# HGRN2's f, q, g and the two gates' projections in seven block products, with the quadrant sums of the input made at HGRN2's start

## The chip, the cores and the metric

The kernel runs on one core of one Trainium2 chip. The metric is the device time of one execution in microseconds (us), the median of several runs. TensorE (PE) does the matmuls and the transposes, VectorE (DVE) and ScalarE (ACT) the elementwise work, GpSimd (POOL) a few small or spare ones, and SyncE (SP) issues all DMAs in one queue, in order.

## The reference, cut to what matters

One block of a network on 512 tokens of width 1024: a SwiGLU feed-forward stage (FFN1), then two mixers side by side on the same normalized input n, HGRN2 (a gated linear recurrence of 8 heads) and a Mamba-2 SSD, joined by two sigmoid gates, then a second feed-forward stage (FFN2), an embedding gate and a norm. What the change touches:

```python
n = rms_norm(h, mix_norm[l])
hq, hf, hi, hgate, mz, mxbc, mdt, br_gates = jnp.split(n @ w_in[l], split_at, axis=-1)
o_hg = hgrn2_recurrence(hq, hf, hi, lower_bounds[l])
o_hg = rms_norm(o_hg, hg_norm[l].reshape(HG_HEADS, HG_DV)).reshape(b_, s_, HG_VDIM)
o_hg = (o_hg * jax.nn.silu(hgate.astype(f32))).astype(h.dtype)
...
gate_a, gate_b = jnp.split(jax.nn.sigmoid(br_gates), 2, axis=-1)
mixed = gate_a * (o_hg @ w_hg_out[l]) + gate_b * (y @ w_ssm_out[l])
h = h + mixed @ w_out[l]
```

hq, hf and hgate (q, f and g below) are 1024 columns each, br_gates 2048. All of it is float32.

## The kernel before

**Matmuls.** Every float32 operand is kept as a pair of float32r blocks, hi and lo. `split` makes the pair: an ACT cast (L507) for hi and a DVE subtraction (L508) for lo. `mm` makes three matmuls of it, hi·hi, hi·lo and lo·hi (L502 to L504). Weights come by DMA (L458) in chunks and are split on the chip, each once; the normalized input n2 is split once and stays (class `Act`).

**Two forms of a projection.** f, q, g, the two gates GA and GB, and ho (the product with `w_hg_out`) use `tile`: 128 output columns by all 512 tokens, eight steps over D = 1024, so 24 matmuls of 128x512 into one PSUM bank. FFN1 and FFN2 use `Seven` instead: four such tiles are computed together as a 2 by 2 block product in seven products of quadrants instead of eight (Strassen and Winograd's form). The seven are a·e, b·g, S4·h, d·T4, S1·T1, S2·T2 and S3·T3, where a, b, c, d are quadrants of the weights, e, f, g, h of the input, S1 to S4 are sums of weight quadrants that DVE makes for each group (L492 to L495, each 128x1024), and T1 to T4 sums of input quadrants that are made once. A product has 24 matmuls of 128x256. `take` gathers the seven results: ACT copies (L851) and DVE adds (L854, L858, L861). A group of `Seven` also has seven weight blocks to split where four tiles have four.

**Order.** `Block.run` goes through a list of units in order. Each unit first loads and splits the weights of units ahead, as far as its six numbers (`AHEAD`, `AHEAD_GATES`, ...: two distances in units of work, one for raw loads, and the blocks to leave spare for each) and the free blocks of the SBUF arena allow (48 blocks, 46 of them of 4 KB a partition). Then it issues its matmuls, and after each piece of them a step of every background generator (`slot`). `pair_gen` is such a generator: the elementwise work and small matmuls of one pair of heads, with decay factors made on POOL (L1243 to L1252), the factored operands on DVE (L1281 to L1284), attention blocks (L1296, L1298, L1305), state (L1316), norm (L1326 to L1332) and a transpose (L1338) that DVE multiplies by the gate (L1339). Each engine executes its instructions in the order that results, and waits on semaphores of the others.

**The stages.** After the SSD's last part come HGRN2's four head pairs: the value projection v (for two pairs at once), then f, q, g of each pair (`HG.plan`; copied out of PSUM by ACT at L1192), then eight tiles of GA (sigmoid L1477), eight of GB (sigmoid L1483, product L1484) and eight of ho (L1491, L1492 and a split), then `w_out` and FFN2.

## Time and profile before

| | us |
|---|---|
| median of 3 runs | 1606.13 (1604.15 to 1610.71) |
| the profiled execution, its own time | 1607.06 |
| its span, first to last instruction | 1605.4 |
| PE busy in the span | 1567.4 (98%) |
| DVE busy | 1001.5 (62%) |
| ACT busy | 717.5 (45%) |
| POOL busy | 203.8 (13%) |

The mean granted TensorE clock of the core is 0.992. ACT's copies of f, q and g (L1192) start between 794.8 and 1010.3 us; the gates run from about 1011 to 1117 us, ho to 1157 us. "Busy" of an engine is the time in which at least one of its instructions executes; a row of a timeline or a group carries the engine, the line of the kernel, the operation, what it writes and reads, and what it waited for in square brackets. Neighbouring instructions on an engine overlap in part, so the cost of one in a row of many is the distance of two starts, not its duration.

### The profile page before, as it was taken

What the parts mean: (1) busy time and instruction counts of PE and PEld (TensorE: products, weight loads), DVE (VectorE), ACT (ScalarE), POOL (GpSimd) and SP (SyncE); (2) the same over time, 40 slices, a digit from 0 to 9 for tenths busy, and PEclk for the clock granted to TensorE, in tenths of its full rate; (3) what the DMA queues carried; (4) which work ended last, traced back from release to release, by engine and by line L of the source; (5) the groups of instructions that cost most, each with busy time, mean ns of one, the idle gap of its engine ahead of it and who ended that gap; (6) DMA issues with size and microseconds to landing.
All of it is one profiled execution on the core that took longest, in us unless ns stands there. A gap on an engine that the chain in (4) does not pass through costs nothing.

```text
span 1605.4 us, 22240 instructions
## 1 busy us (share of the span) xinstructions
PE 1567.4 (98%) x9054; PEld 1362.4 (85%) x9054; DVE 1001.5 (62%) x1223; ACT 717.5 (45%) x1070; POOL 203.8 (13%) x258
## 2 busy tenths in 40 slices
PE   8999999999999899999999999999999999999997
PEld 7999999988877678787878887888889999999986
DVE  7877767665565455667445652644448876877653
ACT  6544544445453444354454353433136543444532
POOL 1000000000044241536211010200000000000000
...
GB/s 272 138 92 108 117 92 79 106 178 189 60 80 63 128 101 142 111 222 100 138 67 112 163 46 48 119 143 92 103 70 116 118 119 80 109 102 85 211 47 53
DMA packets 192044, 181.48 MB, mean 113 GB/s; under 512 B 6804, under 2 KB 155940, under 8 KB 191940
## 3 DMA queue, kind: packets, MB, share of 16 engines
...
HBM read 165.27 MB, written 14.75 MB: 112 GB/s over the span
## 4 chain that ended last, share of the span: by engine, by line
PE 88%; DMA 3%; DVE 3%; POOL 2%; issue 2%; ACT 1%; SPq 0%; POOLq 0%; DVEq 0%; ACTq 0%
PE bank L502 27%; PE bank L504 27%; PE bank L503 27%; DMA blk<-cscr 1%; PE bank L1076 1%; PE bank L1296 1%; PE bank L529 1%; DMA accscr<-blk 1%; DMA blk<-in_x_dram 1%; ACT blk L507 0%; DMA blk<-in_w_in_dram 0%; DVE blk L508 0%; POOL blk L1057 0%; PE bank L1070 0%; POOL blk L1061 0%
## 5 line engine op out<-in xcount | busy, mean ns | idle before, releaser
L502 PE MATMUL bank<-blk,blk 128*128 128x512 f32 (+1 forms) x2648 | 912.3, 347 | 18.2 <-DVE blk L508 9.2
L503 PE MATMUL bank<-blk,blk 128*128 128x512 f32 (+1 forms) x2648 | 909.4, 344 | 0.8 <-DVE blk L508 0.8
L504 PE MATMUL bank<-blk,blk 128*128 128x512 f32 (+1 forms) x2648 | 905.0, 344 | 0.0
L508 DVE TENSOR_TENSOR blk<-blk,blk 128x1024 fp32r<-128x1024 f32 (+2 forms) x461 | 457.3, 1017 | 252.2 <-ACT blk L507 148.2
L502 PEld LDWEIGHTS bank<-blk,blk 128*128 128x128 f32 x2648 | 503.8, 191 | 76.7 <-DVE blk L508 10.5
L507 ACT CAST blk<-blk 128x1024 fp32r<-128x1024 f32 (+2 forms) x461 | 389.6, 879 | 368.0 <-PE bank L503 100.7
L503 PEld LDWEIGHTS bank<-blk,blk 128*128 128x128 f32 x2648 | 504.6, 191 | 55.3 <-DVE blk L508 1.0
L504 PEld LDWEIGHTS bank<-blk,blk 128*128 128x128 f32 x2648 | 502.4, 190 | 53.5 <-issue 0.2
L538 POOL TENSOR_SCALAR small<-small 128x1 f32<-128x1 f32 (+1 forms) x40 | 9.9, 248 | 992.3 <-ACT blk L544 859.3
L851 ACT COPY blk<-bank 128x512 f32<-128x512 f32 x80 | 46.9, 586 | 129.0 <-PE bank L504 129.0
L739 DVE SCALAR_TENSOR_TENSOR blk<-bank,blk 128x512 f32<-128x512 f32 x80 | 54.9, 686 | 30.1 <-PE bank L504 29.5
L955 DVE SCALAR_TENSOR_TENSOR blk<-bank,small,blk 128x511 f32<-128x511 f32 (+2 forms) x72 | 53.6, 744 | 15.8 <-ACT blk L953 14.8
L1076 PEld LDWEIGHTS bank<-blk,blk 128*128 128x128 f32 x256 | 42.4, 198 | 9.1 <-issue 5.5
L1036 DVE TENSOR_TENSOR blk<-blk,blk 128x1024 f32<-128x1024 f32 x16 | 22.9, 1432 | 39.5 <-POOL blk L1034 39.5
L492 DVE TENSOR_TENSOR blk<-blk,blk 128x1024 f32<-128x1024 f32 x20 | 24.4, 1221 | 30.6 <-PE bank L503 15.6
L507 ACT CAST blk<-bank 128x256 fp32r<-128x256 f32 x68 | 23.4, 374 | 35.8 <-PE bank L529 35.6
L1076 PE MATMUL bank<-blk,blk 128*128 128x64 f32 x256 | 38.3, 264 | 0.0
L508 DVE TENSOR_TENSOR blk<-bank,blk 128x256 fp32r<-128x256 f32 x68 | 26.9, 417 | 14.1 <-ACT blk L507 13.8
L731 ACT ACTIVATE blk<-blk 128x512 f32<-128x512 f32 x40 | 25.2, 630 | 20.7 <-DVE blk L854 15.1
L1112 DVE SCALAR_TENSOR_TENSOR blk<-blk,small,blk 128x512 f32<-128x512 f32 x16 | 14.8, 926 | 30.1 <-POOL small L539 20.9
L1037 ACT ACTIVATE blk<-blk 128x1024 f32<-128x1024 f32 x16 | 17.0, 1061 | 36.6 <-DVE blk L1036 32.8
L1034 POOL TENSOR_SCALAR_AFFINE_SELECT blk<-blk 128x1024 f32<-128x1024 f32 x16 | 21.2, 1323 | 95.2 <-DMA blk<-cscr 94.4
...
## 6 DMA issues: line engine op xcount, KB each, us to landing
blk<-in_ffn_w_dram SPq DMA_DIRECT2D x132, 512.0 KB, 4.4
blk<-in_w_in_dram SPq DMA_DIRECT2D x89, 512.0 KB, 3.8
blk<-in_w_ssm_out_dram SPq DMA_DIRECT2D x16, 512.0 KB, 3.9
blk<-cscr SPq DMA_DIRECT2D x16, 512.0 KB, 6.0
...
blk<-in_w_hg_out_dram SPq DMA_DIRECT2D x8, 512.0 KB, 3.5
blk<-in_w_out_dram SPq DMA_DIRECT2D x8, 512.0 KB, 3.9
```

The source lines that it names most:

```text
L492: v.tensor_tensor(s["S1"], q["c"], q["d"], ALU.add)
L502: t.matmul(out, lhsT=lh, rhs=rh, start=start, stop=False, skip_group_check=more)
L503: t.matmul(out, lhsT=lh, rhs=rl, start=False, stop=False, skip_group_check=more)
L504: t.matmul(out, lhsT=ll, rhs=rh, start=False, stop=stop, skip_group_check=more)
L507: self.nc.scalar.copy(hi, src)
L508: self.nc.vector.tensor_tensor(lo, src, hi.bitcast(F32), ALU.subtract)
L731: act(c, c, AF.Silu)
L739: v.scalar_tensor_tensor(hd, bank, 0.5, hd, ALU.mult, ALU.add)
L851: b.nc.scalar.copy(st[p], bank)
L955: nc.vector.scalar_tensor_tensor(t[:, s:], pc[:, 0:T - s], b.cw[:, 3 - s, ct:ct + 1], t[:, s:], ALU.mult, ALU.add)
L1036: v.tensor_tensor(R[j], R[j], self.cc[:, j, gh][:, :, None].broadcast_to([P, HPG, P]), ALU.subtract)
L1076: nc.tensor.matmul(pyv[:, hh, :], lhsT=R[c][:, hh, :], rhs=xdt[:, hh, :], start=True, stop=True)
```

## The change

- **T1 to T4 for n2.** `ActS`, a new class, adds the four sums of n2's quadrants as operand pairs: eight more blocks that stay until the gates end. The generator `sums` makes them as HGRN2 begins, from the pairs that are there (four additions of 128x1024, eight subtractions of 128x512 and eight splits of 128x512). Before that, `KEEP` = 8 blocks are held free (`reserve`).
- **f, q, g.** f and q of a pair are one group of `Seven`, g of two pairs another: six groups instead of 24 tiles. A pair's generator starts when all four of its inputs are there.
- **The gates.** Two tiles of GA and the two of GB with the same place form a group: four groups instead of 16 tiles. `gates_done` works on halves of the tokens (256), and so does `ho_done`.
- **Lookahead.** HGRN2's units get (6, 10, 16, 2, 4, 4) and the gates' and ho's (6, 10, 16, 2, 3, 3).

Ten groups of `Seven` take the place of 40 tiles. Weights, loads and results are the same in number and size, but a load is now half the depth by 256 columns (128x4x256). Lines of helpers move down by 37 to 41 (L502 to L504 become L539 to L541, L507 and L508 L544 and L545, L492 to L495 L529 to L532, L458 L495).

```diff
-AHEAD_GATES = (2, 6, 8, 4, 8, 8)
+AHEAD_HG = (6, 10, 16, 2, 4, 4)
+AHEAD_GATES = (6, 10, 16, 2, 3, 3)
...
+class ActS(Act):
+    def sums(self):
+        b, v = self.b, self.b.nc.vector
+        self.op = {k: b.pair(4, T // 2) for k in ("T1", "T2", "T3", "T4")}
+        b.reserve = 0
+        for i in range(2):
+            full = []
+            for hi, lo in (self.blocks[i], self.blocks[i + 2]):
+                full.append(b.t(2, T))
+                v.tensor_tensor(full[-1], hi.bitcast(F32), lo.bitcast(F32), ALU.add)
+            yield 1
...
+            for r, x, y, n in ((t, h, f, "T3"), (f, f, e, "T1"), (f, h, f, "T2"), (g, g, f, "T4")):
+                v.tensor_tensor(r, x, y, ALU.subtract)
+                b.split(r, *[z[:, 2 * i:2 * i + 2] for z in self.op[n]])
...
+    def seven(self, w, c0, c1, act, done, pace):
+        ch = Chunk(w, 0, KD, c0, 4 * P, "w", c1)
+        q = Seven(self, act, done)
+        return [Unit([next(x for x in ch.halves if x.j == PRODUCTS[p][0])], lambda wt, p=p: q.product(wt, p, pace))
+                for p in ORDER]
...
-        for nme, off in (("f", OFF_F), ("q", OFF_Q), ("g", OFF_G)):
-            res += b.tiles(Chunk(b.i["w_in"], 0, KD, off + hp * 256, 256, "c"), self.n,
-                           lambda j, bank, nme=nme: made(j, bank, nme), HG_PACE)
+        res += b.seven(w, OFF_F + hp * 256, OFF_Q + hp * 256, self.n, made((st, "f"), (st, "q")), HG_PACE)
+        if hp % 2 == 0:
+            nxt = self.st[hp + 1]
+            res += b.seven(w, OFF_G + hp * 256, OFF_G + hp * 256 + 256, self.n, made((st, "g"), (nxt, "g")), HG_PACE)
...
     def hg_begin():
         hg.begin()
+        b.start("sums", n2[0].sums())
...
+    def gates_done(o, A, d):
+        for j in range(2):
+            acc[d + j] = b.t(T)
+            nc.sync.dma_start(acc[d + j], ssd.scr_acc[d + j])
+        for th in range(2):
+            nc.scalar.activation(o[th], o[th], AF.Sigmoid)
+            s_[d, th] = o[th]
+        for th, y in ((1, o[3]), (0, None)):
+            x = b.t(2, 256) if y is None else y
+            nc.scalar.activation(x, A if y is None else y, AF.Sigmoid)
+            for j in range(2):
+                a = acc[d + j][:, th * 256:th * 256 + 256]
+                nc.vector.tensor_tensor(a, a, x[:, j], ALU.mult)
+            b.fr(x)
...
+    for d in range(0, KD, 2):
+        U.extend(b.seven(ins["w_in"], OFF_GA + d * P, OFF_GB + d * P, n2, lambda o, A, d=d: gates_done(o, A, d), GATE_PACE))
```

**DVE, where the gates begin and the last pair of heads (6 and 7) is worked on.** A row is the line, the operation, what it writes and reads, the size, and the engines that it waits for. Before, this is the pair's chain from an L1284 on, with two weight splits (the L508 of 128x1024):

```order
L1284 TENSOR_TENSOR blk4_6226<-blk8_6755,small_63 128x512 [waits DVE_49,Pool_49]
L1330 TENSOR_REDUCE small_63<-blk6_6379 128x4 [waits Activation_49]
L1283 TENSOR_TENSOR blk5_7563<-blk16_7433,small_63 128x384 [waits PE_49]
L1284 TENSOR_TENSOR blk5_7563<-blk8_6755,small_63 128x512
L1257 SCALAR_TENSOR_TENSOR blk11_7136<-blk11_7136,blk10_7268 128x1024 [waits Activation_49]
L1332 TENSOR_TENSOR blk6_6379<-bank1_65,small_63 128x512 [waits DVE_49,Pool_49]
L508 TENSOR_TENSOR blk35_6496<-blk18_7133,blk26_6938 128x1024 [waits DMAHW2_49,PE_49,Activation_49]
L508 TENSOR_TENSOR blk7_7270<-blk10_7268,blk19_6497 128x1024 [waits DMAHW3_49,PE_49,Activation_49]
L1339 SCALAR_TENSOR_TENSOR blk6_6379<-bank4_68,small_63,blk36_6868 128x512 [waits DVE_49,PE_49]
L1283 TENSOR_TENSOR blk36_6868<-blk16_7433,small_63 128x384 [waits DVE_49]
L508 TENSOR_TENSOR blk21_7052<-blk6_6379,blk21_7052 128x512 [waits Activation_49]
```

In the changed kernel the chain begins at the transposed head (L1395) and runs to the split of a group's S1 (`blk23_7791`, an addition made 29 rows earlier), the lo part of which is `blk46_8081`:

```order
L1395 SCALAR_TENSOR_TENSOR blk26_7018<-bank2_66,small_63,blk46_7197 128x512 [waits DVE_49,PE_49]
L1284 TENSOR_TENSOR blk37_8024<-blk20_8002 128x1024 [waits DVE_49]
L1285 TENSOR_TENSOR blk27_8023<-blk20_8002 128x1024
L545 TENSOR_TENSOR blk21_8062<-blk26_7018,blk21_8062 128x512 [waits Activation_49]
L1310 TENSOR_TENSOR blk37_8024<-blk37_8024,blk17_7473 128x1024 [waits Activation_49]
L1311 SCALAR_TENSOR_TENSOR blk20_8002<-blk20_8002,blk5_7716 128x1024 [waits Activation_49]
L1337 TENSOR_TENSOR blk41_174<-blk37_8024,small_63 128x512 [waits DVE_49,Pool_49]
L1337 TENSOR_TENSOR blk1_6543<-blk37_8024,small_63 128x512
L1312 TENSOR_TENSOR blk15_7682<-blk15_7682,blk17_7473 128x1024 [waits Activation_49]
L1340 TENSOR_TENSOR blk1_6543<-blk20_8002,small_63 128x512 [waits DVE_49,Pool_49]
L545 TENSOR_TENSOR blk46_8081<-blk23_7791,blk26_8080 128x1024 [waits Activation_49]
```

More of the pair's chain now stands between a read of PE's transposes and the next weight split: ten operations ahead of the split of S1 here, where two weight splits came right behind L1257 and L1332 before.

**PE, at the same place.** Before, one split of a weight block (`blk7_7270` is the lo part) is followed by 24 matmuls of 128x512; these are the last of the tile before and the first of it:

```order
L504 MATMUL bank6_70<-blk29_1940,blk35_6496 128x512
L502 MATMUL bank7_71<-blk45_3214,blk19_6497 128x512
L503 MATMUL bank7_71<-blk42_3215,blk19_6497 128x512
L504 MATMUL bank7_71<-blk45_3214,blk7_7270 128x512
L502 MATMUL bank7_71<-blk45_3214,blk19_6497 128x512
L503 MATMUL bank7_71<-blk42_3215,blk19_6497 128x512
L504 MATMUL bank7_71<-blk45_3214,blk7_7270 128x512
L502 MATMUL bank7_71<-blk24_2460,blk19_6497 128x512
L503 MATMUL bank7_71<-blk28_122,blk19_6497 128x512
```

In the changed kernel, from the transposes that DVE's L1395 reads (`bank2_66`) to the first matmul that reads `blk46_8081`; the rows left out are eleven matmuls of 128x256 of lines L539 to L541 that wait for nothing:

```order
L1394 MATMUL bank2_66<-small_63,blk26_7018 128x128 [waits DVE_49]
L1394 MATMUL bank2_66<-small_63,blk26_7018 128x128 x3
L541 MATMUL bank1_65<-blk13_104,blk35_7957 128x256
L539 MATMUL bank1_65<-blk13_104,blk18_5830 128x256
...
L539 MATMUL bank1_65<-blk47_5006,blk34_7353 128x256 [waits Activation_49]
L540 MATMUL bank1_65<-blk4_4974,blk34_7353 128x256
L1352 MATMUL bank6_70<-blk20_8002,blk37_8024 32x32 [waits DVE_49]
L539 MATMUL bank4_68<-blk3_1180,blk26_8080 128x256 [waits Activation_49]
L540 MATMUL bank4_68<-blk7_4870,blk26_8080 128x256
L1347 MATMUL bank5_69<-small_63,blk41_174 128x128 [waits DVE_49]
L1347 MATMUL bank5_69<-small_63,blk41_174 128x128 x2
L541 MATMUL bank4_68<-blk3_1180,blk46_8081 128x256 [waits DVE_49]
```

Between the two stand 17 matmuls of 128x256, one of 32x32 and three transposes of 128x128.

**SP, in the gates.** Before, four weight loads and the two loads of `accscr` stand so:

```order
L1479 DMA blk12_7580<-accscr_118 128x512 [waits PE_49]
L458 DMA blk18_7133<-in_w_in_dram 128x8x128 [waits Pool_49]
L458 DMA blk10_7268<-in_w_in_dram 128x8x128 [waits DMAHW3_49,DVE_49]
L458 DMA blk18_7133<-in_w_in_dram 128x8x128 [waits DMAHW4_49,DMAHW2_49,DVE_49]
L1479 DMA blk17_5245<-accscr_118 128x512 [waits DMAHW5_49,PE_49]
L458 DMA blk10_7268<-in_w_in_dram 128x8x128 [waits DMAHW6_49,DMAHW3_49,DVE_49]
L458 DMA blk6_6379<-in_w_in_dram 128x8x128 [waits DMAHW7_49,DVE_49]
```

In the changed kernel the load into `blk44_7676` waits for DVE's L1395 that reads this block as its gate operand:

```order
L1541 DMA blk12_3228<-accscr_118 128x512 [waits DMAHW6_49,DVE_49,PE_49]
L1573 DMA blk1_6543<-hscr_73 128x1024 [waits DMAHW7_49]
L495 DMA blk44_7676<-in_w_in_dram 128x4x256 [waits DMAHW0_49,DVE_49,Pool_49]
L495 DMA blk23_7791<-in_w_in_dram 128x4x256 [waits DMAHW1_49,DVE_49,PE_49]
L1541 DMA blk41_174<-accscr_118 128x512 [waits DMAHW2_49,DVE_49]
L495 DMA blk35_8651<-in_w_in_dram 128x4x256 [waits DMAHW3_49,PE_49]
```

On DVE, that L1395 and the addition of the next group that needs the load stand three rows apart:

```order
L902 TENSOR_TENSOR blk15_7682<-blk15_7682,bank4_68 128x512 [waits PE_49,Activation_49]
L1395 SCALAR_TENSOR_TENSOR blk23_7791<-bank3_67,small_63,blk44_7676 128x512 [waits DVE_49,PE_49]
L545 TENSOR_TENSOR blk43_8120<-blk23_7791,blk43_8120 128x512 [waits Activation_49]
L899 TENSOR_TENSOR blk25_5100<-blk25_5100,blk41_174 128x512 [waits Activation_49]
L529 TENSOR_TENSOR blk46_8525<-blk0_7476,blk44_7676 128x1024 [waits DMAHW6_49,DMAHW0_49]
L1550 TENSOR_TENSOR blk12_3228<-blk12_3228,blk25_5100 128x256 [waits DMAHW6_49,Activation_49]
L530 TENSOR_TENSOR blk0_7476<-blk0_7476 128x1024 [waits DVE_49]
```

The load and its user stand on either side of the same few DVE instructions.

## Rows read from the trace of the kernel before

**Rows 1.** The profile's page: busy time of each engine, share of the span, instructions.

```profile
PE 1567.4 (98%) x9054; PEld 1362.4 (85%) x9054; DVE 1001.5 (62%) x1223; ACT 717.5 (45%) x1070; POOL 203.8 (13%) x258
```

**Rows 2.** Windows: stretch, length, busy time per engine (instructions), granted clock, DMA share, GB/s.

```profile
794.00:1011.00 217.00, 217.00 (x1106) 176.45 (x1105) 111.95 (x139) 104.58 (x150) 32.84 (x54) 1.00 0.28 84
1011.00:1117.00 106.00, 105.83 (x525) 87.69 (x524) 47.31 (x56) 35.69 (x53) 8.33 (x7) 1.00 0.45 131
130.00:340.00 210.00, 210.00 (x1491) 198.22 (x1491) 149.24 (x174) 97.30 (x133) 0.00 (x0) 1.00 0.36 112
880.00:900.00 20.00, 20.00 (x110) 16.56 (x109) 20.00 (x27) 11.74 (x16) 0.02 (x1) 1.00 0.63 197
```

**Rows 3.** Timeline of PE in ho: start, duration, engine, line, operation, operands, tile, shape.

```profile
1120.10 0.39 PE L502 MATMUL bank<-blk,blk 128*128 128x512 f32 x1
...
1125.54 0.39 PE L502 MATMUL bank<-blk,blk 128*128 128x512 f32 x1
```

**Rows 4.** Timeline of PE in FFN1, a group of Seven.

```profile
103.59 0.28 PE L502 MATMUL bank<-blk,blk 128*128 128x256 f32 x1
...
107.43 0.28 PE L504 MATMUL bank<-blk,blk 128*128 128x256 f32 x1
```

**Rows 5.** DVE's groups by line and shape: count, busy, mean ns, idle before.

```profile
L508 DVE TENSOR_TENSOR blk<-blk,blk 128x1024 fp32r<-128x1024 f32 x321 | 393.3, 1235 | 242.4 <-ACT blk L507 138.7 <-PE bank L503 48.4 <-issue 20.6
...
L492 DVE TENSOR_TENSOR blk<-blk,blk 128x1024 f32<-128x1024 f32 x20 | 24.4, 1221 | 30.6 <-PE bank L503 15.6 <-PE bank L504 10.5 <-DMA blk<-in_ffn_w_dram 4.0
...
L854 DVE TENSOR_TENSOR blk<-blk,bank 128x512 f32<-128x512 f32 x20 | 13.6, 682 | 3.7 <-PE bank L504 3.7
```

**Rows 6.** ACT's groups by line and shape: casts of weights, copies of Seven's take.

```profile
L507 ACT CAST blk<-blk 128x1024 fp32r<-128x1024 f32 x321 | 332.5, 1050 | 305.7 <-PE bank L503 100.7 <-DMA blk<-in_w_in_dram 87.8 <-PE bank L504 30.5
L851 ACT COPY blk<-bank 128x512 f32<-128x512 f32 x80 | 46.9, 586 | 129.0 <-PE bank L504 129.0
```

**Rows 7.** Timeline of DVE in FFN1, two of the weight sums.

```profile
120.97 1.23 DVE L493 TENSOR_TENSOR blk<-blk,blk 128x1024 f32<-128x1024 f32 x1
122.23 1.23 DVE L494 TENSOR_TENSOR blk<-blk,blk 128x1024 f32<-128x1024 f32 x1
```

**Rows 8.** Timeline of DVE in HGRN2, the elementwise chain of a pair.

```profile
877.59 0.75 DVE L1339 SCALAR_TENSOR_TENSOR blk<-bank,small,blk 128x512 f32<-128x512 f32 x1
878.37 2.73 DVE L1228 TENSOR_TENSOR blk<-blk 128x1024 f32<-128x1024 f32 x1
...
886.24 0.68 DVE L1281 TENSOR_TENSOR blk<-blk,small 128x512 f32<-128x512 f32 x1
886.84 0.42 DVE L1282 TENSOR_TENSOR blk<-blk,small 128x256 f32<-128x256 f32 x1
...
890.78 1.22 DVE L1256 TENSOR_TENSOR blk<-blk,blk 128x1024 f32<-128x1024 f32 x1
891.92 1.22 DVE L1257 SCALAR_TENSOR_TENSOR blk<-blk,blk 128x1024 f32<-128x1024 f32 x1
```

**Rows 9.** Timeline of POOL beside the L1228 of the group above.

```profile
877.62 2.40 POOL L1211 TENSOR_TENSOR blk<-blk,blk 128x1024 f32<-128x1024 f32 x1 [3.60 <-ACT blk L1210]
```

**Rows 10.** Timeline of DVE as the gates begin, two of its weight splits.

```profile
1021.44 1.22 DVE L508 TENSOR_TENSOR blk<-blk,blk 128x1024 fp32r<-128x1024 f32 x1 [0.95 <-ACT blk L507]
1024.82 1.22 DVE L508 TENSOR_TENSOR blk<-blk,blk 128x1024 fp32r<-128x1024 f32 x1 [2.15 <-ACT blk L507]
```

**Rows 11.** The page's DMA issues: count, size, us from issue to landing.

```profile
blk<-in_w_in_dram SPq DMA_DIRECT2D x89, 512.0 KB, 3.8
```

**Rows 12.** Timeline of PE at its longest wait for DVE.

```profile
529.17 0.80 PE L502 MATMUL bank<-blk,blk 128*128 128x512 f32 x1 [6.66 <-DVE blk L508]
```

**Rows 13.** Windows around that wait, columns as in group 2.

```profile
528.00:532.00 4.00, 2.83 (x7) 2.26 (x8) 3.67 (x7) 2.26 (x4) 0.00 (x0) 0.50 0.00 0
532.00:536.00 4.00, 4.00 (x17) 3.29 (x16) 1.39 (x2) 1.92 (x2) 0.00 (x0) 0.88 0.00 0
```

102 lines of the change are left out of this document (61 added, 41 removed).

## The prediction

> **What bounds the kernel now.** The page's busy times come first: PE is busy for 98% of the span, DVE for 62%, ACT for 45% [rows 1]. Shares of a whole span hide stages, so the windows come next [rows 2]. In the stretch in which f, q and g are made (794 to 1011 us) PE is busy for all 217.00 us and DVE for 111.95; in the gates (1011 to 1117 us) PE is busy for 105.83 of 106 us and DVE for 47.31. PE alone sets the time of both stages, and whatever takes matmul time away there is a gain until another engine ends last. FFN1, which already uses the seven products, shows the other side: between 130 and 340 us PE is busy for all 210.00 us with DVE at 149.24 us, 71%. Even a stretch with DVE busy for all of its 20.00 us (880 to 900 us) leaves PE busy for all 20.00. So DVE may be very busy without PE's waiting, as long as what it makes is made early enough. The question is therefore where the order leaves no such room.
>
> The sum is made on the profiled execution of 1607.06 us, which lies 0.93 us above the median of the three runs; the result is brought down by that at the end. A measurement of this kernel tells from no change what differs by about 0.5%, 8.0 us: below 1598.1 us is faster, above 1614.2 us slower.
>
> **The change part by part: PE.** From 1120.10 to 1125.54 us PE starts 24 matmuls of 128x512: 5.44 us, 0.2267 us each [rows 3]. From 103.59 to 107.43 us it starts 32 of 128x256: 3.84 us, 0.120 us each [rows 4]. Four tiles are 96 x 0.2267 = 21.76 us, a group of seven products 168 x 0.120 = 20.16 us: 1.60 us saved, not the 2.72 us that an eighth would be, since a matmul of half the width costs 53% of a full one. Ten groups: **-16.0 us**. The evictions of PSUM, PE's transposes and the recurrence's matmuls stay as they were.
>
> The Trainium skill, "TensorE: Matmul & The Clock Gate", section "Back-to-back issue gap", gives an isolated gap of N/2.4 + 2.5 ns: by its formula 109.2 and 215.8 ns here. This would be an estimate of 2.37 us a group and 23.7 us in all; the trace's 120 and 226.7 ns are longer at both widths, and they decide.
>
> **DVE and ACT, on average.** Each group adds on DVE four weight sums, 1.26 us from start to start in FFN1 [rows 7], 5.0 us; three more splits of 128x1024 (seven instead of four), which take 1.22 to 1.24 us each [rows 5] and 1.14 us from start to start in a dense row, as L1256 to L1257 shows for the same shape [rows 8], 3.4 us; and three additions of `take`, 0.68 us each [rows 5] or 0.60 from start to start [rows 8], 1.8 us. That is 10.2 us a group. Six groups bring the first stage from 111.95 to 173.2 us in 217 - 9.6 = 207.4 us (84%); four bring the gates from 47.31 to 88.1 in 106 - 6.4 = 99.6 us (88%). The sums of n2's quadrants are four operations of 128x1024 and sixteen of 128x512, 4 x 1.14 + 16 x 0.60 = 14.2 us, once; with all of them in the first stage it would be at 90%. I cost them at nothing: they are handed out as PE runs the SSD's last part and the value projection, and the first group is the first that needs them; without that cover they cost up to 14.2 us. ACT gets three more casts at 1.05 us and four copies at 0.586 us in each group [rows 6], 5.5 us, and reaches 137.6 of 207.4 us and 57.7 of 99.6: no bound, costed at nothing. The evictions and the gates' sigmoids and products are cut in halves or doubled in width at about the same time. The loads keep their number and size.
>
> **DVE, at the densest place.** 84 to 90% is more than FFN1's 71%, so I looked in the order for the place where PE must wait however far DVE was ahead. It is at the start of the gates, where the last pair of heads is worked on. DVE's L1395 reads transposes that PE makes at that time, so DVE cannot be ahead of PE there; and PE needs the split of S1 that stands ten operations behind it. By the rows of group 8 (and the 0.60 us of a 128x512): L1395 0.78, L1284 and L1285 2.28, the split of 128x512 0.60, L1310 and L1311 2.28, two L1337 1.20, L1312 1.14, L1340 0.60, and the S1 split to its end 1.22 [rows 8]. Together 10.1 us. PE has 17 matmuls of 128x256 between its transposes and the one that reads the split, 2.0 us, and four smaller ones for which I take the same price, 0.5 us. It waits 10.1 - 2.5 = **+7.6 us**, and nothing in the order hides that. Before, the two splits of this stretch were waiting for ACT (0.95 and 2.15 us of idle time), so DVE had time to spare [rows 10], and each served 24 matmuls of 128x512, 5.44 us; a split now serves 24 of 128x256, 2.88 us. It can be dearer: an L1228 that ran beside POOL's L1211 of 2.40 us took 2.73 us instead of 1.14 [rows 8, 9], and the new chain has two operations of that kind, so 1.6 us more stay as an upper bound.
>
> The Trainium skill, "GPSIMD Engine Reference", section "8. Key points", says that GpSimd shares its SBUF interfaces with VectorE and contends with DVE instructions that have two SBUF inputs. The 2.73 us agree with this, and it speaks against a change that adds such instructions to stages in which POOL works; for the sum it would be those 1.6 us.
>
> **A load between two DVE instructions.** In the gates the load into `blk44_7676` waits for an L1395 on DVE, and the addition of the next group, three rows behind it, waits for the load. A weight load lands 3.8 us after its issue [rows 11]; DVE has a split and an addition of 128x512 in between, 1.2 us. DVE then waits 2.6 us, with all that is queued behind that addition. I found four such places; as DVE may have got ahead of PE again, I count one, **+2.6 us**, with 0 and 10.4 as bounds.
>
> **The clock.** After PE's longest wait for DVE, 6.66 us [rows 12], the granted clock of the window was 0.50 (1.2 GHz) and 0.88 in the next 4 us [rows 13]. From 529.17 to 532 us half of 2.83 us is lost, then 12% of 4 us: **+1.9 us** for a wait of such a length; 0 and 3.8 (two such waits) are the bounds.
>
> **Sum.** -16.0 + 7.6 + 2.6 + 1.9 = -3.9 us: 1603.2 us on the profiled execution, 1602.3 against the median. With the bounds: 7.6 alone gives 1598.7 - 0.9 = 1597.8, and 7.6 + 1.6 + 10.4 + 3.8 = 23.4 gives 1614.5 - 0.9 = 1613.6.
>
> **The rivals.**
> - **A, all of the gain.** DVE is never late for PE: 1607.06 - 16.0 - 0.9 = 1590 us. For it speak FFN1 at 71% and the window with DVE at 100%, both without a wait of PE [rows 2]. Against it speaks that the chain of the densest place starts at PE itself. Chance 0.18. If matmuls were spaced closer than in rows 3 and 4, by the ratio of their widths (0.113 us for the half), it would be 27 us, and 1579 without waits or 1591 with mine; chance 0.04. The Trainium skill's formula, above, is of this kind: 1582 as an estimate without waits.
> - **B, the forecast.** Most of the gain goes into one long wait at the gates' start and some smaller ones: 1602, between 1598 and 1614. Chance 0.52.
> - **C, slower: loads chained to DVE.** T1 to T4 hold eight of the 46 small blocks until the gates end, so a load often finds its block still in use by a DVE instruction, and DVE soon needs what is loaded. Each such round trip costs 3.8 - 1.2 = 2.6 us. If eight of the gates' sixteen loads are so and PE feels each, that is 20.8 instead of 2.6 us: 1602.3 + 18.2 = 1620 us. It decides from six felt round trips on: with 7.6 and 1.9 us they make 25.1 us, 9 more than PE saves. DVE at 88% speaks for it, since little time is left to get ahead in again; against it that FFN1 holds as many operands and loads at the same rate without a wait. Chance 0.22.
> - **D, the quadrant sums are late.** The first group needs all of T1 to T4; if none were ready, PE would wait for 14.2 us of DVE: 1616 us. Chance 0.04.
>
> **How the numbers follow.** The likeliest is B: 1602 us. A and C lie at 1590 and 1620, with 0.18 and 0.22; a range from 1590 to 1620 takes in B with its bounds, and about half of each of A and C. Faster: A with its variant, 0.22, and the lowest edge of B, 0.04: 0.26. Slower: most of C and half of D: 0.24. Within 0.5%: 0.50.
>
> **What would show it.** Right: PE's busy time falls by about 16 us less the time at half clock; the first stage has hardly a wait; one wait of PE of 7 us or more for a DVE split (L545) stands at the start of the gates, near the last pair's L1312 and L1340, with a granted clock under 1 behind it; DVE's share is 80 to 90% in both stages. A would show PE without gaps in the gates, C many waits of 1 to 4 us there with DVE idle for loads of `w_in`, D a wait ahead of the first group. Wrong would be a matmul of 128x256 in these stages at other than 0.12 us, or a pair's chain on DVE that takes less than the 10.1 us from L1395 to the S1 split.

## The result, and the profile after

The changed kernel takes 1634.66 us (median of 6 runs, 1632.27 to 1641.67), the kernel before 1608.14 in the same comparison: a ratio of 1.0174, 95% interval 1.0151 to 1.0197. It is slower by 28 us by the ratio (26.5 between the medians), where 1602 was forecast and 1590 to 1620 given as the range. The profiled execution has a span of 1632.0 us, 26.6 more than before.

The page answers [rows 1] with these lines: busy time of PE, PEld, DVE, ACT and POOL, and the clock granted to PE in 40 slices.

```profile
PE 1570.7 (96%) x9774; PEld 1402.0 (86%) x9774; DVE 1119.1 (69%) x1375; ACT 769.3 (47%) x1154; POOL 222.6 (14%) x258
PEclk9999999999999999999999999799999999999999
```

PE is busy for 3.3 us more than before although its work is 16 us less, and it is idle for 1632.0 - 1570.7 = 61.3 us instead of 38.0. The view of the cores has the other half: the mean granted clock fell from 0.992 to 0.979. With (1 - clock) x span as the time lost to half clock, that is 34.3 us instead of 12.8. So **+23.3 us idle, +21.5 us at half clock, -16.0 us of work** make +28.8, where the span has +26.6. The two losses overlap a little, since a wait in a stretch at half clock counts in both.

The stages, as windows (columns as in [rows 2]): the SSD's last part, HGRN2, the gates, and ho.

```profile
700.00:795.00 95.00, 88.49 (x412) 70.94 (x411) 72.77 (x81) 35.76 (x59) 39.42 (x34) 0.96 0.39 121
795.00:1016.00 221.00, 213.09 (x1544) 197.07 (x1542) 165.37 (x187) 129.55 (x191) 43.82 (x47) 0.98 0.30 96
1016.00:1144.60 128.60, 115.01 (x836) 108.56 (x837) 94.17 (x114) 68.63 (x98) 12.21 (x18) 0.92 0.37 115
1144.60:1183.00 38.40, 38.40 (x182) 32.26 (x182) 25.43 (x58) 13.09 (x24) 0.00 (x0) 1.00 0.30 98
```

Before, the first stage ended some 11 us earlier; PE was idle for 1.60 us in it, for nothing in the second and 0.17 us in the third, and the clock was 1.00 in all of them. Now PE is idle for 6.5, 7.9 and 13.6 us in the first three, 28.0 us together, and the clock is below 1 in each. DVE is at 75% of the second stage and 73% of the third, less than the 84 and 88% of the forecast, mostly because the stages became longer; DVE's averages do not explain the waits.

The waits of PE, one list for each of these three stages (what waits, for whom, us in total, times, longest):

```profile
PE bank L1117 <- POOL blk L1098: 2.5, 2, 1.9
PE bank L1115 <- POOL blk L1102: 1.9, 2, 1.3
PE bank L566 <- DVE blk L1153: 1.3, 1, 1.3
...
PE bank L1352 <- DVE blk L1311: 2.2, 1, 2.2
PE bank L541 <- DVE blk L545: 2.0, 1, 2.0
PE bank L540 <- DVE blk L545: 1.8, 1, 1.8
...
PE bank L539 <- ACT blk L892: 5.9, 4, 2.6
PE bank L541 <- DVE blk L545: 3.4, 3, 2.3
PE bank L1352 <- DVE blk L1311: 2.7, 1, 2.7
```

The first three lines are the SSD's own steps (no group of Seven has begun there, but the quadrant sums are made there), the next three stand in HGRN2 (a pair's attention block that waits for a factor, and two matmuls that wait for a weight split), the last three in the gates. In the gates the largest item is one that the forecast does not have: PE waits for ACT's copy in `take` (L892). Products 1, 6, 7 and 4 of a group gather in one bank, so product 6 cannot start until ACT has copied product 1 out, and only product 2 (2.88 us) stands between them; product 7 waits for the copy of product 6 in the same way. A tile had no such tie.

The place on which the forecast rested, the start of the gates, as timelines of DVE (first two lines) and of PE:

```profile
1030.34 0.73 DVE L1395 SCALAR_TENSOR_TENSOR blk<-bank,small,blk 128x512 f32<-128x512 f32 x1
...
1040.02 1.21 DVE L545 TENSOR_TENSOR blk<-blk,blk 128x1024 fp32r<-128x1024 f32 x1
```

```profile
1033.72 0.58 PE L539 MATMUL bank<-blk,blk 128*128 128x256 f32 x1 [2.60 <-ACT blk L892]
...
1037.19 0.32 PE L1352 MATMUL bank<-blk,blk 128*32 128x32 f32 x2 [2.68 <-DVE blk L1311]
...
1041.29 0.58 PE L541 MATMUL bank<-blk,blk 128*128 128x256 f32 x1 [2.34 <-DVE blk L545]
```

From L1395 to the end of the S1 split DVE takes 10.89 us (10.1 were forecast, and 0.73 of it is a wait for ACT). PE waits 2.60 + 2.68 + 2.34 = 7.62 us meanwhile; 7.6 were forecast, as one wait for a DVE split. Of the three waits that came, the first ends with ACT's copy and the other two, 5.02 us, with DVE's chain. The windows of the same place show what else it costs (the clock is the third number from the right):

```profile
1028.00:1032.00 4.00, 3.12 (x27) 2.91 (x25) 3.12 (x4) 3.95 (x5) 0.00 (x0) 1.00 0.00 0
1032.00:1036.00 4.00, 0.80 (x2) 0.50 (x2) 3.27 (x5) 3.99 (x7) 3.26 (x9) 0.67 0.01 2
1036.00:1040.00 4.00, 1.75 (x7) 1.22 (x7) 4.00 (x5) 2.41 (x3) 1.14 (x2) 0.50 0.00 0
1040.00:1044.00 4.00, 2.71 (x12) 2.71 (x13) 4.00 (x6) 0.00 (x0) 0.00 (x0) 0.50 0.00 0
1044.00:1048.00 4.00, 4.00 (x24) 3.84 (x22) 3.48 (x6) 1.91 (x3) 0.00 (x0) 0.62 0.00 0
```

From 1033 to 1047 us PE is granted half its clock. The matmuls' price, on the other hand, is right: in the gates at full clock these two are 37 starts apart, 4.44 us, 0.120 us each.

```profile
1080.08 0.28 PE L539 MATMUL bank<-blk,blk 128*128 128x256 f32 x1
...
1084.52 0.28 PE L540 MATMUL bank<-blk,blk 128*128 128x256 f32 x1
```

### The profile page after: what moved, and what is told of

It reads as the page before. It is cut to its first block, busy times and chain, and to the rows that moved or that the text cites. A ratio compares the mean times of both kernels' runs of the same rounds, so it can differ in the third digit from the quotient of the medians.

```text
span 1632.0 us, 23951 instructions
## 1 busy us (share of the span) xinstructions
PE 1570.7 (96%) x9774; PEld 1402.0 (86%) x9774; DVE 1119.1 (69%) x1375; ACT 769.3 (47%) x1154; POOL 222.6 (14%) x258
## 4 chain that ended last, share of the span: by engine, by line
PE 81%; DMA 5%; DVE 4%; ACT 4%; issue 3%; POOL 3%; SPq 0%; POOLq 0%; DVEq 0%; ACTq 0%
PE bank L539 25%; PE bank L540 25%; PE bank L541 25%; DMA blk<-cscr 1%; DVE blk L545 1%; ACT blk L544 1%; PE bank L1352 1%; PE bank L1117 1%; DMA accscr<-blk 1%; PE bank L566 1%; POOL blk L1098 1%; DMA blk<-in_x_dram 1%; POOL blk L1102 1%; DMA blk<-in_w_in_dram 1%; POOL blk L1075 0%
## 5 line engine op out<-in xcount | busy, mean ns | idle before, releaser
L539 PE MATMUL bank<-blk,blk 128*128 128x256 f32 (+1 forms) x2888 | 948.1, 331 | 22.9 <-DVE blk L545 6.9
L540 PE MATMUL bank<-blk,blk 128*128 128x256 f32 (+1 forms) x2888 | 946.8, 329 | 2.6 <-DVE blk L545 2.6
L541 PE MATMUL bank<-blk,blk 128*128 128x256 f32 (+1 forms) x2888 | 939.3, 328 | 5.4 <-DVE blk L545 5.4
L545 DVE TENSOR_TENSOR blk<-blk,blk 128x1024 fp32r<-128x1024 f32 (+2 forms) x507 | 504.5, 1021 | 188.8 <-ACT blk L544 122.4
L539 PEld LDWEIGHTS bank<-blk,blk 128*128 128x128 f32 x2888 | 555.0, 193 | 72.6 <-DVE blk L545 8.2
L540 PEld LDWEIGHTS bank<-blk,blk 128*128 128x128 f32 x2888 | 556.3, 193 | 46.4 <-DVE blk L545 3.3
L541 PEld LDWEIGHTS bank<-blk,blk 128*128 128x128 f32 x2888 | 553.4, 193 | 49.2 <-DVE blk L545 6.4
L544 ACT CAST blk<-blk 128x1024 fp32r<-128x1024 f32 (+2 forms) x507 | 425.5, 874 | 335.0 <-PE bank L540 86.6
L575 POOL TENSOR_SCALAR small<-small 128x1 f32<-128x1 f32 (+1 forms) x40 | 14.1, 354 | 975.2 <-ACT blk L581 858.0
L892 ACT COPY blk<-bank 128x512 f32<-128x512 f32 x120 | 70.0, 585 | 154.2 <-PE bank L541 149.7
L529 DVE TENSOR_TENSOR blk<-blk,blk 128x1024 f32<-128x1024 f32 x30 | 36.7, 1222 | 44.5 <-PE bank L540 15.6
L996 DVE SCALAR_TENSOR_TENSOR blk<-bank,small,blk 128x511 f32<-128x511 f32 (+2 forms) x72 | 53.5, 744 | 11.2 <-ACT blk L994 10.2
L1117 PEld LDWEIGHTS bank<-blk,blk 128*128 128x128 f32 x256 | 42.0, 206 | 12.7 <-issue 6.3
L1077 DVE TENSOR_TENSOR blk<-blk,blk 128x1024 f32<-128x1024 f32 x16 | 23.7, 1483 | 36.4 <-POOL blk L1075 36.4
L544 ACT CAST blk<-bank 128x256 fp32r<-128x256 f32 x68 | 23.5, 374 | 37.5 <-PE bank L566 34.6
L530 DVE TENSOR_TENSOR blk<-blk,blk 128x1024 f32<-128x1024 f32 x29 | 36.4, 1255 | 3.3 <-DMA blk<-in_ffn_w_dram 2.2
L545 DVE TENSOR_TENSOR blk<-bank,blk 128x256 fp32r<-128x256 f32 x68 | 27.0, 418 | 14.6 <-ACT blk L544 14.5
L531 DVE TENSOR_TENSOR blk<-blk,blk 128x1024 f32<-128x1024 f32 x30 | 36.6, 1220 | 0.4
L1075 POOL TENSOR_SCALAR_AFFINE_SELECT blk<-blk 128x1024 f32<-128x1024 f32 x16 | 23.3, 1459 | 97.7 <-DMA blk<-cscr 95.8
```

What stands on the lines that cost most here:

```text
L529: v.tensor_tensor(s["S1"], q["c"], q["d"], ALU.add)
L530: v.tensor_tensor(s["S3"], q["a"], q["c"], ALU.subtract)
L531: v.tensor_tensor(s["S2"], s["S1"], q["a"], ALU.subtract)
L539: t.matmul(out, lhsT=lh, rhs=rh, start=start, stop=False, skip_group_check=more)
L540: t.matmul(out, lhsT=lh, rhs=rl, start=False, stop=False, skip_group_check=more)
L541: t.matmul(out, lhsT=ll, rhs=rh, start=False, stop=stop, skip_group_check=more)
```

## The experiments

Each kernel was run beside the kernel before, and the ratio is to it. The table holds each profiled execution against that of the kernel before: PE idle is span less PE busy, clock is (1 - mean clock) x span, work is 1.60 us for each group of Seven; all are differences in us. The ratio rests on 4 to 10 executions of a kernel, the columns from idle to span on one. One is a sample: the six executions of e17 have mean clocks of 0.982 to 0.990, which is 29 to 16 us at half clock, and the profiled one is the fastest of them, as that of e16 is of its four.

| kernel | groups | ratio (95% interval) | idle | clock | work | sum | span |
|---|---|---|---|---|---|---|---|
| the change | 10 | 1.0174 (1.0151 to 1.0197) | +23.3 | +21.5 | -16.0 | +28.8 | +26.6 |
| e1 sums only | 0 | 1.0078 (1.0051 to 1.0104) | +3.5 | +6.6 | 0 | +10.1 | +10.3 |
| e5 blocks only | 0 | 1.0069 (1.0049 to 1.0088) | +4.1 | +4.9 | 0 | +9.0 | +7.5 |
| e9 lookahead only | 0 | 1.0071 (1.0053 to 1.0089) | +4.7 | +11.5 | 0 | +16.2 | +15.6 |
| e13 pace, a control | 0 | 1.0007 (0.9990 to 1.0025) | -2.5 | +1.7 | 0 | -0.8 | +2.2 |
| e2 HGRN2 only | 6 | 1.0120 (1.0091 to 1.0148) | +22.4 | +13.3 | -9.6 | +26.1 | +23.5 |
| e3 gates only | 4 | 1.0080 (1.0055 to 1.0105) | +10.5 | +13.1 | -6.4 | +17.2 | +15.1 |
| e4 one weight sum | 10 | 1.0115 (1.0090 to 1.0140) | +24.8 | +16.5 | -16.0 | +25.3 | +23.3 |
| e7 pace 1.0 | 10 | 1.0134 (1.0100 to 1.0167) | +30.5 | +10.0 | -16.0 | +24.5 | +20.2 |
| e10 sigmoids written later | 10 | 1.0136 (1.0114 to 1.0158) | +21.8 | +21.4 | -16.0 | +27.2 | +24.6 |
| e16 sigmoids bound later | 10 | 1.0150 (1.0110 to 1.0191) | +25.2 | +11.6 | -16.0 | +20.8 | +20.1 |
| e6 sums in the middle | 7 | 1.0080 (1.0051 to 1.0109) | +17.0 | +9.9 | -11.2 | +15.7 | +14.1 |
| e8 the same, pace 1.0 | 7 | 1.0073 (1.0044 to 1.0102) | +13.2 | +14.7 | -11.2 | +16.7 | +14.8 |
| e11 e8, old lookahead for tiles | 7 | 1.0072 (1.0055 to 1.0089) | +13.0 | +13.1 | -11.2 | +14.9 | +15.0 |
| e12 e11, sigmoids written later | 7 | 1.0056 (1.0041 to 1.0071) | +12.4 | +13.1 | -11.2 | +14.3 | +12.9 |
| e17 e11, sigmoids bound later | 7 | 1.0063 (1.0040 to 1.0086) | +14.6 | +3.3 | -11.2 | +6.7 | +8.0 |
| e14 gates, late sums | 4 | 1.0118 (1.0089 to 1.0147) | +17.0 | +16.6 | -6.4 | +27.2 | +25.5 |
| e15 e14, sigmoids written later | 4 | 1.0051 (1.0030 to 1.0073) | +15.2 | +9.9 | -6.4 | +18.7 | +16.2 |
| e18 gates, earlier sums, bound | 4 | 1.0053 (1.0037 to 1.0069) | +8.5 | +8.2 | -6.4 | +10.3 | +9.2 |

In all nineteen the sum comes within 4.3 us of the span, in seventeen within 2.6. Busy and idle time make up the span by definition; what the agreement shows is that PE's busy time changed by the work saved and the time at half clock, and by little else. What is left to find is where the idle time and the half clock come from. Where a run is held against its expectation below, its time is the ratio times 1608.14 us.

### How much is there without any group of Seven?

**e1, the sums alone.** In the changed kernel f, q, g and the gates go back to tiles, and all lookahead numbers to those of before; `sums` stays.

```diff
-        res += b.seven(w, OFF_F + hp * 256, OFF_Q + hp * 256, self.n, made((st, "f"), (st, "q")), HG_PACE)
+        for nme, off in (("f", OFF_F), ("q", OFF_Q), ("g", OFF_G)):
+            res += b.tiles(Chunk(b.i["w_in"], 0, KD, off + hp * 256, 256, "c"), self.n,
+                           lambda j, bank, nme=nme: made(j, bank, nme), HG_PACE)
```

> All projections in the tiles of before; only the quadrant sums T1 to T4 are made at HGRN2's start and kept, unused, until the gates end (eight blocks). Theory P (each place where PE waits costs its wait and about as much again at half clock, and the places are the SSD's tail for the sums, the pairs' chains and the gates' start): the sums alone cost the 9 us by which the SSD's last matmul lags in the changed kernel, so about 1617 us. Theory Q (DVE's load: every group of Seven loses about the same, the sums are small): 1608, no change. Theory R (the eight blocks starve the lookahead): most of the loss is already here, over 1625.

1.0078, some 12 us (1621; theory P's 1617 is the nearest): what was costed at nothing costs over two fifths as much as the whole change. **e5** keeps e1's eight blocks and leaves out the sums' work:

```diff
         self.op = {k: b.pair(4, T // 2) for k in ("T1", "T2", "T3", "T4")}
         b.reserve = 0
-        for i in range(2):
-            ...
+        yield 1
```

> As the kernel with the quadrant sums alone, but only their eight blocks are taken and held until the gates end; nothing is computed into them and every projection is in tiles. If the 10 us of that kernel come from the sums' work on DVE and ACT during the SSD's last part, this is about 1608 us plus what the chip differs by, no change; if they come from the blocks that later loads miss, it is as slow as that kernel, +8 to +12 us.

1.0069: as slow as with the sums, within the intervals, but not at the same place. The sums' additions start on DVE between 704 and 757 us in e1 and between 704 and 762 us in the changed kernel, among the SSD's own steps. The windows from 744 to 784 us, of the kernel before, the changed kernel, e1 and e5 in this order:

```profile
744.00:784.00 40.00, 38.40 (x198) 30.82 (x197) 25.17 (x33) 12.57 (x21) 19.86 (x20) 1.00 0.39 119
744.00:784.00 40.00, 33.49 (x147) 25.39 (x147) 34.43 (x34) 12.26 (x19) 31.54 (x24) 0.91 0.34 108
744.00:784.00 40.00, 33.17 (x149) 25.44 (x148) 33.77 (x36) 16.20 (x25) 26.70 (x21) 0.91 0.61 187
744.00:784.00 40.00, 40.00 (x205) 32.23 (x205) 24.30 (x30) 14.31 (x23) 23.50 (x21) 1.00 0.65 191
```

With the sums' work DVE is busy for 34 of the 40 us and PE idle for 6.5 and 6.8; with the blocks alone PE has no gap. The same holds for every kernel of the table: the eight that make the sums there (the change, e1, e2, e3, e4, e7, e10, e16) have PE idle for 3.5 to 7.3 us in this window, the kernel before and the other eleven for 0 to 1.6. So the sums' work makes the SSD's waits, and the blocks by themselves cost elsewhere: e5's two longest waits are in pairs' chains, where nothing of the change computes. The equal totals of e1 and e5 stand for different losses. The first of e5's two waits on PE's timeline:

```profile
892.86 0.25 PE L1323 MATMUL bank<-blk,blk 128*32 128x32 f32 x2 [2.58 <-DVE blk L1282]
```

**e9** takes the kernel before and changes its HGRN2 lookahead alone:

```diff
-        u.ahead, u.pack = (AHEAD_SSD if i < ssd1 else AHEAD), PACK_MIX
+        u.ahead, u.pack = (AHEAD_SSD if i < ssd1 else (6, 10, 16, 2, 4, 4)), PACK_MIX
```

> The kernel before with one change: its HGRN2 units get the changed kernel's lookahead numbers (6, 10, 16, 2, 4, 4) instead of (4, 8, 10, 4, 8, 8). No sums, no blocks, no Seven. In the two kernels with the sums between the pairs PE waits 7 us for ACT's work of the SSD at 725 to 742 us, before anything of the change has run there, with 6.8 us at half clock. If the lookahead (more weight splits pulled ahead of the SSD's own work) makes these, this is +7 to +10 us; if the blocks held free make them, no change.

1.0071, 11 us, a little over what the lookahead theory had, with these waits of PE in the SSD's last part:

```profile
727.68 0.66 PE L1003 MATMUL bank<-small,blk 128*128 128x128 f32 x4 [3.10 <-ACT blk L957]
...
742.35 0.46 PE L1042 MATMUL bank<-blk,blk 128*128 128x128 f32 x2 [2.64 <-ACT blk L880]
```

**e13** asks whether any change of the order would do this (`HG_PACE` 1.6 instead of 1.75 in the kernel before).

> The kernel before with one number changed: 1.6 instead of 1.75 background steps per tile of f, q and g. No sums, no blocks, no Seven, no other lookahead; only where the steps of the pairs and of the SSD's end fall among the tiles. If any shift of the order costs some 10 us, because the order of before is one in which nothing is late, it loses as much as the kernels with the sums, the blocks or the lookahead alone: +6 to +12 us. If those three lose for reasons of their own (fewer blocks, more weights ahead), this is level, within 3 us.

1.0007: level, with no stretch at half clock between 700 and 1600 us. So this shift of the steps costs nothing; eight blocks less, or a longer reach ahead with fewer blocks to spare, each cost 11 us by themselves. How a missing block makes a pair's chain late was not followed further. The waits of e9 (for ACT, 725 to 745 us) are found again in e6 and e8, which have the new lookahead too, but not in the changed kernel; what the lookahead costs there no run shows.

### Which groups, and is it DVE's load?

**e2** has Seven in HGRN2 and tiles in the gates, **e3** the reverse (with `KEEP` 12). The lookahead goes with the groups: e2 has the new one for HGRN2 and the old one for the gates and ho, e3 the reverse.

> Six groups of Seven in HGRN2, the gates in tiles as before. Theory P: 9 us for the sums, and for the HGRN2 stage waits of 7.8 us, 5 us of half clock and 9.6 us of gain, together +12: 1620 us. Theory Q: six tenths of the 27 us, 1624. Theory R: 1630 or more.

> Four groups of Seven in the gates, f, q and g in tiles as before, 12 blocks instead of 8 held free before the sums are made. Theory P: 9 us for the sums and 16 for the gates (13.5 us of waits, 9 us of half clock, 6.4 us of gain): 1633 us. Theory Q: four tenths of 27 us, 1619. Theory R: 1630 or more.

Beside the sums alone (12 us), e2 is 7 us worse and e3 no worse. The 7 us need not come from e2's six groups: its lookahead alone made 11 us in e9. The places theory (P) has neither number: it had 12 us for e2 (19 measured, 15 to 24 by the interval) and 25 for e3 (13 measured, 9 to 17). The load theory (Q) had 16 and 11, both within the intervals, though its small sums do not fit e1. Beside e1 the gates' four groups cost nothing more (e3), beside e2 they cost 9 us more (the change): what they cost depends on what stands ahead of them, and that was not followed further.

**e4** tests the load: it leaves out three of the four weight sums of each group, so that f, q, g and the gates come from other weights, and takes some 36 us of DVE work out (1119.1 to 1082.7 us busy):

```diff
             v.tensor_tensor(s["S1"], q["c"], q["d"], ALU.add)
+            if c.w is self.i["w_in"]:
+                return c.sums[j]
             v.tensor_tensor(s["S3"], q["a"], q["c"], ALU.subtract)
```

> The changed kernel with three of the four weight sums of each of its ten groups left out (the bare quadrants are used in their place, so f, q, g and the gates are computed from other weights): 30 operations of 1.26 us, 38 us of DVE time less. Theory P: the chain from L1395 to the split of S1 has none of these sums in it, so the wait at the gates' start stays, and what goes is part of the others: 1622 to 1630 us. Theory Q: the load is back near FFN1's share, nearly the whole loss and perhaps the gain come back: 1600 to 1612.

1.0115, 1627 us, in theory P's range and far from Q's: about a third of the loss comes back, the rest does not, and PE's waits at the gates' start are those of the changed kernel (lines are 3 higher):

```profile
1033.67 0.39 PE L542 MATMUL bank<-blk,blk 128*128 128x256 f32 x1 [2.60 <-ACT blk L895]
...
1037.04 0.31 PE L1355 MATMUL bank<-blk,blk 128*32 128x32 f32 x2 [2.87 <-DVE blk L1314]
...
1041.15 0.58 PE L544 MATMUL bank<-blk,blk 128*128 128x256 f32 x1 [2.26 <-DVE blk L548]
```

DVE's total load is not the cause there; the chain is, as forecast.

### What binds at the gates' start?

A product unit (2.88 us of PE) hands out 1.75 background steps, as a tile unit (5.44 us) does, so a pair's chain passes in half the PE time. **e7** sets 1.0 (and `KEEP` 12):

```diff
-        U.extend(b.seven(..., lambda o, A, d=d: gates_done(o, A, d), GATE_PACE))
+        U.extend(b.seven(..., lambda o, A, d=d: gates_done(o, A, d), 1.0))
```

> The changed kernel with the step rate of its ten groups set from 1.75 to 1.0 steps of the background generators per product (12 blocks held free instead of 8 before the sums). A tile unit is 5.44 us of PE and hands out 1.75 steps, a product unit 2.88 us and hands out 1.75 as well, so a pair's chain stands in PE's queue at half the distance in PE time; at 1.0 it is what it was before. Step-rate theory: the waits in the pairs' chains and at the gates' start (18 us with 14 us of half clock) mostly go and the sums' 10 us stay: 1605 to 1613 us. Chain theory (the chain on DVE is 10 us however the steps are set, and PE's part of it grows only from 2.5 to 4.4 us): 1622 to 1630.

1.0134 and 1630 us, at the upper end of the chain theory's range. The waits change shape and stay:

```profile
1034.13 1.08 PE L1394 MATMUL bank<-small,blk 128*128 128x128 f32 x4 [6.15 <-ACT small L1286]
...
1039.24 0.32 PE L1352 MATMUL bank<-blk,blk 128*32 128x32 f32 x2 [4.03 <-DVE blk L1311]
```

In the changed kernel ACT executes the first group's sigmoid between the pair's Ln and Exp there, with two table loads of 1.28 us. **e10** writes the gates' sigmoids as a generator that waits for the last pair.

> The changed kernel with the gates' sigmoids, products and loads of partial sums put off until the last pair of heads is done (a copy out of the bank takes the place of the sigmoid). At the gates' start ACT loads its table twice (1.28 us each) between the pair's Ln and Exp, for one sigmoid of the first group. If ACT binds there, the 4 us of waits for the copy and part of the 5 us for DVE's chain go, with some of the half clock: 1624 to 1630 us. If DVE's chain alone binds (10 us however ACT does), 1632 to 1636, as the changed kernel.

1.0136 (1630 us, where the first range ends), but the run says nothing on table loads: ACT's timeline still has the sigmoid (L1549) between Ln (L1273) and Exp (L1286). A later place in the program did not move it on the engine.

```profile
1030.52 0.82 ACT L1273 ACTIVATE blk<-blk,small 128x512 f32<-128x512 f32 x1
1031.35 1.28 ACT L1549 ACT_TABLE_LOAD   x1
1032.65 0.63 ACT L1549 ACTIVATE blk<-blk 128x512 f32<-128x512 f32 x1
1033.30 1.28 ACT L1286 ACT_TABLE_LOAD   x1
```

**e16** makes the sigmoids depend on the last head:

```diff
+            nc.vector.tensor_scalar(zero[0], hg.out.k[HEADS_H - 1][0].bitcast(F32)[:, 0:1], 0.0, 0.0, ALU.mult, ALU.add)
...
-            nc.scalar.activation(o[th], o[th], AF.Sigmoid)
+            nc.scalar.activation(o[th], o[th], AF.Sigmoid, bias=zero[0])
```

> The changed kernel with the gates' sigmoids bound to the last head's result (a zero made from it is their bias), so that they can't come before the last pair is done. In the run that only wrote them later ACT still executed the first one between the pair's Ln and Exp, with its two table loads. If ACT's order binds at the gates' start: two loads of 1.28 us and the sigmoid of 0.6 go, the 2.6 us wait for the copy and some 2 of the 5 us for DVE's chain with the half clock: 1624 to 1630 us. If DVE's chain alone binds: 1631 to 1636, as the changed kernel.

The loads are gone from that place, the wait for the copy falls from 2.60 to 1.19 us, and the time does not come back: PE waits more for the chain.

```profile
1028.67 0.38 PE L539 MATMUL bank<-blk,blk 128*128 128x256 f32 x1 [1.19 <-ACT blk L892]
...
1032.65 0.31 PE L1352 MATMUL bank<-blk,blk 128*32 128x32 f32 x2 [3.48 <-DVE blk L1311]
1037.10 0.58 PE L541 MATMUL bank<-blk,blk 128*128 128x256 f32 x1 [2.59 <-DVE blk L545]
```

These are 7.26 us, against 7.62, and 6.07 of them are now for DVE. Its median of 1632.24 us lies in the chain theory's 1631 to 1636, and DVE's chain binds at this place. (The intervals of the two ratios overlap; a gain of 2 to 4 us is neither shown nor excluded.)

### Is there a version that gains?

**e6, e8, e11, e12, e17** keep the first two pairs in tiles and make the sums between them (`b.start("sums", ...)` after `hg.plan(0)`). e8 adds 1.0 steps, e11 the old lookahead for all units but groups, e12 and e17 the sigmoids of e10 and of e16.

> f, q and g of the first two pairs in tiles as before, the sums made between the first and the second pair instead of at HGRN2's start, the other pairs and the gates in Seven (seven groups, 11.2 us of gain). Places theory (each wait costs itself and about as much at half clock): the SSD's 10 us and the waits of the first two pairs (5 us and three stretches of 3.4 us at half clock) go, the gates' start stays with 11 us of waits and 10 of half clock: +10, about 1618 us. Load theory: 1625. If the sums cost the same wherever they are: 1628.

> Both: first two pairs in tiles, sums between the first and the second pair, 1.0 steps per product in the seven groups that are left. Step-rate theory: 11.2 us of gain, small waits, 1598 to 1606 us, faster than the kernel before by 2 to 10 us. Chain theory: 1610 to 1616.

> As the kernel with the sums between the first and second pair and 1.0 steps, with the new lookahead for the groups of Seven alone and the old one for the value projections, the SSD's last units and the tiles of the first two pairs. Lookahead theory: its 7 us of waits and 5 of half clock before 745 us go: 1609 to 1613. If they come from something else, 1620 again.

> The one above with the gates' sigmoids put off as well. If ACT's table loads bind at the gates' start (3.8 us of waits for a cast behind three loads): 3 to 6 us less than the one above, 1604 to 1609 us, level with the kernel before. If DVE's chain binds, equal to the one above.

> The kernel with sums between the first and second pair, 1.0 steps, the old lookahead for tiles, and the sigmoids bound as above. Its largest wait (5.0 us for a group's copy on ACT behind an Exp that waits for DVE's scan, in the third pair) has no sigmoid in it and stays: 1614 to 1618, as the kernel in which they were only written later. Under 1608 if the gates' sigmoids were what cost there.

All lie between 1.0056 and 1.0080. e6 (1621 us) lies between its theories' 1618 and 1625, e8 (1620) above both of its ranges, e11 (1620) outside the lookahead theory's 1609 to 1613, e12 is level with e11 within the intervals, as it should be if DVE's chain binds, and e17 (1618) is at the top of its 1614 to 1618. In e11 the SSD's 6 to 7 us of waits did fall to 1.5, as the lookahead theory said, but the total stayed: the third pair's chain now holds a group's copy back. On ACT's timeline an Exp (L1299, with its table load) waits 4.13 us for DVE's scan, and the copy stands behind it. First ACT, then PE:

```profile
984.77 1.28 ACT L1299 ACT_TABLE_LOAD   x1 [4.13 <-DVE blk L1291]
...
988.12 0.56 ACT L892 COPY blk<-bank 128x512 f32<-128x512 f32 x1
```

```profile
988.74 0.58 PE L539 MATMUL bank<-blk,blk 128*128 128x256 f32 x1 [5.02 <-ACT blk L892]
```

**e14, e15, e18** have Seven in the gates alone, with 1.0 steps and the arena's two large blocks kept free from then on. e14 makes the sums as the last pair begins, e15 adds e10's edit, e18 makes them one pair earlier and adds e16's.

> All of HGRN2 in tiles and in the order of before until the last pair; the quadrant sums are made as the last pair begins, the gates in Seven at 1.0 steps per product (6.4 us of gain). Nothing before about 950 us is moved. Theory that the order's shift is what costs: no wait before 950, the gates' start keeps some 8 us of waits and 7 of half clock with the last pair's chain: 1608 + 15 - 6 = about 1615. If the gates' groups are harmless where nothing ahead of them is moved: 1602 to 1606, faster than before.

> The one above with the gates' sigmoids put off until the last pair is done. ACT's queue theory (a group's copy out of PSUM, for which PE waits, stands in ACT's order behind table loads and the pair's activations): 3 to 6 us less than the one above, 1609 to 1612. DVE chain theory: equal to the one above.

> f, q and g in tiles as before, the sums at the third pair (one pair earlier than in the kernel with 8.4 us of waiting for the first gate group's weights), gates in Seven at 1.0 steps with bound sigmoids: 6.4 us of gain. If the long wait came from the sums, the group's weight sums and the last pair's chain standing in one row on DVE, it goes: 1604 to 1610, level with or a little under the kernel before. If it is the gates' start itself, 1616 to 1620.

1.0118 (1627 us, above both of e14's expectations), 1.0051 (1616) and 1.0053 (1617, in the range for "the gates' start itself"). In e14, as in e15, the first group's weight sums, other splits and the last pair's scan stand in one row on DVE, and PE waits for the first weights that are a sum, S2 (the first of these timelines of PE, e14). The quadrant sums are not in that row, as e18's expectation supposed: in e14 the last of their subtractions starts at 985 us, 32 us before this wait begins. In e18 this wait is 3.71 us (the second timeline), but a wait of 4.07 us for DVE stands at 1065.70 us instead.

```profile
1025.98 0.58 PE L539 MATMUL bank<-blk,blk 128*128 128x256 f32 x1 [8.43 <-ACT blk L544]
```

```profile
1018.51 0.58 PE L541 MATMUL bank<-blk,blk 128*128 128x256 f32 x1 [3.71 <-DVE blk L545]
```

e18 is the cleanest case, four groups with 6.4 us of work saved, and it still has 8.5 us more of idle time and 8.2 more at half clock. No version beat the kernel before; the nearest are 0.5% slower. e15 is 11 us better than e14, where 3 to 6 were expected, with the same wait of 8.43 us: two later waits for casts (2.40 and 4.50 us in e14) are gone. What removed them was not tested; the first sigmoid has the same place on ACT in both.

## Why the prediction was wrong

**PE, -16.0: right.** 0.120 us a matmul in the changed kernel, and the account of nineteen kernels closes with 1.60 us a group. The 109.2 ns by the formula for an isolated matmul in the Trainium skill ("TensorE: Matmul & The Clock Gate", section "Back-to-back issue gap") are below these 120 ns.

**The densest place, +7.6: right in place and mechanism, and in size partly by luck** (7.62 us). e4 and e16 took DVE's other load and ACT's table loads away, and it stayed. But it came as three waits, one of them (2.60 us) for ACT, and two misses cancel: DVE's chain took 0.8 us more than forecast, and so did PE's own part, part of it at half clock. The dearer operations beside POOL (up to 1.6 us) did not come: L1284 and L1285 took 1.22 us each.

**The clock, +1.9 with a bound of 3.8: the first wrong step.** It measured +21.5 us. The forecast priced half clock once, for one wait as long as the 6.66 us of [rows 12, 13], as if shorter waits were free of it. In the changed kernel the clock fell eight times between 700 and 1250 us, six of them at waits of 0.8 to 2.6 us and twice without a wait, and 20.5 us went there; in the kernel before it fell not once in that time. Over the whole kernel half clock cost nearly as much as the waits did, but not wait by wait: four waits of 0.55 to 1.32 us between 766 and 775 us, and single ones of 1.19 and 1.50 us at 939 and 1027 us, were followed by no fall. Nor does the same wait always cost the same. As FFN2 begins, PE waits 0.89 us for a cast and then 0.78 to 0.80 us for a split in all twenty profiled executions; in seven of them the clock fell behind it, in thirteen it did not. The kernel before, then the changed kernel:

```profile
1214.00:1220.00 6.00, 4.79 (x38) 4.59 (x39) 6.00 (x11) 4.01 (x7) 0.00 (x0) 1.00 0.77 239
1239.40:1245.40 6.00, 4.78 (x25) 4.57 (x26) 6.00 (x11) 4.01 (x7) 0.00 (x0) 0.72 0.75 244
```

What decides it stays open.

**The quadrant sums, costed at nothing: the second.** They cost some 12 us alone (e1). The cover named was the SSD's last part and the value projection, in which PE would run on while DVE made them. The first group did not wait for them, so rival D did not come; but in the SSD's last part they stand between DVE's own steps for the SSD, for which PE and POOL wait, and PE was idle there for 6.5 us with the clock at 0.96, where 1.60 us at 1.00 stood before. Without their work (e5) these waits are gone. What was missed besides is that the step holds eight blocks, which cost some 11 us alone (e5); how much of that is in the changed kernel no run shows. Rival C named the blocks, but with a mechanism that was not seen: in the gates PE waited for no load itself, and DVE for 5 us.

**The lookahead numbers: not costed at all.** They stood in the diff, and alone they make 1.0071 (e9); the waits that they make there are not among those of the changed kernel.

**Idle time elsewhere.** The forecast had 10.2 us in the gates, 7.6 + 2.6; the whole is 23.3 us more than before. The load between two DVE instructions (2.6) does appear as 2.7 us of DVE's waiting, but not on PE. In its place stand the SSD's 6.5 us, 7.9 us in HGRN2, and in the gates ACT's copies, 5.9 us (2.60 of them in the 7.62 above): a bank that four products share ties PE to ACT within 2.88 us. ACT was dismissed by its 58 to 66% of busy time, the same reading by averages that the forecast had refused for DVE.

The range failed because its bounds belonged to the places found, and nothing stood for places that were not looked at. Rival C's price, 1620, was nearer than the forecast; its reason was not.
